# A streaming log-sum-exp: twenty loads in place of nineteen, and the rows' sums dealt out again

## The chip, the core and the metric

The kernel runs on one core of one Trainium2 chip. The metric is device time in microseconds (us), the median of several runs. Five engines matter here: SP (SyncE) issues the transfers, ACT (ScalarE) computes the exponentials, DVE (VectorE) and POOL (GpSimd) sum the rows, and PE (TensorE) does three tiny products at the end. Sixteen DMA engines move the data.

## The reference

The input `x` has 32 x 512 = 16,384 rows of 1,024 numbers in float32, 67.1 MB. For every row the log of the sum of the exponentials is wanted:

```
max_x = np.max(x, axis=-1, keepdims=True)
return max_x.squeeze(-1) + np.log(np.sum(np.exp(x - max_x), axis=-1))
```

The kernel leaves the maximum out at first: it sums the plain exponentials, takes the logarithm, and looks at the end whether every sum lies between 1e-15 and 1e15. Only if one does not, a second pass with the maximum is run, which this input does not need.

## The kernel before, in words

**Layout.** Every one of the 128 partitions holds 128 rows, so a "row" below means one row of 1,024 numbers in each partition, 512 KB in all. The rows pass through a ring in SBUF with room for 48 rows (`RING`). The list `LOADS` is the whole plan: each entry is one transfer, with its size in rows (fractions are allowed) and a string that says what is done with the rows that it completes. Sizes of `before` add up to 128 rows in 19 loads, from 15.6 rows at the start to 0.47 at the end.

**The letters.** `R9` means: one exponential over nine rows on ACT (line 229, in place), then one reduction over the nine rows on DVE (line 240, nine sums). `G5` means: the exponential, then POOL adds the two halves of each of the five rows (line 235), and DVE later sums the halves that are left, 512 numbers a row (line 159). `H` is the place in DVE's order at which all such folded rows are summed. `T2` means: for each of two rows one DVE instruction that adds the two halves and accumulates the row's sum (line 167). `a` and `b` are the last row in two pieces: of `a` DVE adds the halves and accumulates, of `b` ACT itself accumulates during the exponential (line 224). `C` is an early range check on DVE over the sums so far (line 176, two reductions), and `L` the logarithm of the first 112 rows on ACT (line 202), which are then stored while the rest is under way. Parts that are joined by `+` share one exponential.

**Head starts.** A load's size and the rows that it completes need not agree. When a load brings more than the rows that its string names, the exponential covers all that has landed, and the remainder waits in the ring for the next load. So the exponential of a later load can be shorter than the rows that it completes.

**Order.** Each engine works through the plan in its written order; semaphores tie them together. ACT waits for a load's landing (line 188), DVE and POOL for ACT's exponential, DVE for POOL's fold. SP issues the loads in order on one queue (line 141, in the helper `load`). Before a load overwrites a place in the ring, SP waits until DVE has summed the rows that lay there (line 138). If the next load does not fit behind the last one, the ring starts again at its beginning. The first load is issued at the very start, ahead of the program's other preparations.

**`HELD`.** For one load (line 245) DVE waits, before its `T` sums, for the landing of the load after it, and executes an empty instruction.

**The end.** After the last sums, ACT takes the logarithms of rows 112 to 126 (line 267) and of the last row (line 269), and copies one value (line 272); SP stores the last 16 rows; DVE looks at the sums that the early check did not see (lines 278 and 282), PE adds it all up (lines 288 to 292), DVE turns it into a truth value (line 296), and ACT and DVE branch on it.

Of the kernel before, what the change touches and what calls it, by code (L numbers as in the profile page):

```python
# [10 lines left out]
RING = 48  # L11
B = 16

HELD = 15

# [2 lines left out]


LOADS = [
# [5 lines left out]
]  # L28


# [23 lines left out]
def kernel(  # L54
# [125 lines left out]
    for i, (size, parts) in enumerate(loads):  # L180
# [8 lines left out]
        for k, part in enumerate(parts):  # L189
# [41 lines left out]
            for how, s in part:  # L231
# [12 lines left out]
                elif how == "T":  # L244
                    if i == HELD:
                        nc.vector.wait_ge(landed[i + 1], 16)
# [161 lines left out]
```

## Time and profile before

| | before |
|---|---|
| median of 3 runs | 161.53 us (161.51 to 161.56) |
| the profiled execution's own time | 161.49 us |
| its span, first to last instruction | 160.2 us |
| DVE busy | 116.2 us (73%) |
| ACT busy | 114.6 us (72%) |
| POOL busy | 33.3 us (21%) |
| HBM read | 67.11 MB |

The span is the time between the first and the last instruction of the program; the profiled execution's own time is 1.3 us longer. All starts below are in us from the span's start. An engine's busy share is an average over the span: ACT and DVE have nothing to do until the first load has landed, at 21.4 us. Where ACT or DVE instructions follow each other directly, the next one starts a little under 0.1 us before the end of the one before, so the step from start to start is a little less than the duration.

### The profile page before, as it was taken

To read this page: it belongs to the slowest core of one execution; us is meant where nothing else is said; L and a number is where in the kernel's file an instruction comes from. 1 tells how busy PE (TensorE), PEld (TensorE's weight loads), DVE (VectorE), ACT (ScalarE), POOL (GpSimd) and SP (SyncE) were. 2 spreads that over 40 slices of the span, in tenths; PEclk is the share of its full clock that TensorE was granted. 3 is DMA by queue.
4 is the path that set the end of the run, shared out by engine and by line. 5 is a ranking of instruction groups with operands and counts; after the bars stand their busy time and mean duration, and the time that the engine had idled before them with its cause. 6 is when DMAs were issued, how large, how long until landed. Compare 5 with 4: busy or idle time off the path is not lost.

```text
span 160.2 us, 183 instructions
## 1 busy us (share of the span) xinstructions
PE 0.3 (0%) x6; PEld 0.2 (0%) x6; DVE 116.2 (73%) x56; ACT 114.6 (72%) x32; POOL 33.3 (21%) x14
## 2 busy tenths in 40 slices
PE   0000000000000000000000000000000000000000
PEld 0000000000000000000000000000000000000000
DVE  0000000029997599999999699929999999999996
ACT  3000069970999419992799349964998999999996
POOL 0000000000000000000000000990580589996000
DMA  8997999799699699996999999997989999999993
GB/s 272 496 512 336 432 515 466 306 515 498 272 513 513 272 479 478 478 463 268 453 468 468 468 430 430 430 430 332 499 364 472 415 446 395 451 395 431 414 408 105
DMA packets 3025, 67.18 MB, mean 419 GB/s; under 512 B 592, under 2 KB 720, under 8 KB 1488
## 3 DMA queue, kind: packets, MB, share of 16 engines
q1 hardware_dynamic: 3024, 67.18, 97.9%
q14 instruction: 1, 0.01, 0.0%
HBM read 67.11 MB, written 0.07 MB: 419 GB/s over the span
## 4 chain that ended last, share of the span: by engine, by line
DMA 53%; ACT 21%; DVE 18%; POOL 5%; issue 0%; PE 0%; SPq 0%
DMA ring<-in_x_dram 53%; ACT ring L229 21%; DVE sumexp L240 15%; POOL ring L235 5%; DVE sumexp L159 2%; ACT ring L224 0%; SPq L141 0%; DVE clamped L278 0%; PE count L288 0%; ACT res L202 0%; DVE fine L296 0%; PE count L290 0%; PE count L292 0%
## 5 line engine op out<-in xcount | busy, mean ns | idle before, releaser
L229 ACT ACTIVATE ring<-ring 128x16000 f32<-128x16000 f32 (+24 forms) x25 | 112.2, 4546 | 42.7 <-DMA ring<-in_x_dram 42.6
L240 DVE TENSOR_REDUCE sumexp<-ring 128x9 f32<-128x9216 f32 (+7 forms) x10 | 89.8, 9000 | 39.1 <-ACT ring L229 39.1
L235 POOL TENSOR_TENSOR ring<-ring 128x2048 f32<-128x2048 f32 (+5 forms) x8 | 33.0, 4128 | 112.3 <-ACT ring L229 112.2
L159 DVE TENSOR_REDUCE sumexp<-ring 128x4 f32<-128x2048 f32 (+5 forms) x8 | 16.5, 2079 | 3.4 <-POOL ring L235 3.4
L167 DVE SCALAR_TENSOR_TENSOR ring<-ring 128x512 f32<-128x512 f32 (+1 forms) x16 | 9.8, 672 | 0.0
L128 ACT ACT_TABLE_LOAD x1 | 1.3, 1283 | 1.4 <-PEq L63 1.4
L167 DVE DVE_READ_ACCUMULATOR ring<-ring 128x1 f32 x16 | 1.3, 82 | 0.0
L224 ACT ACTIVATE ring<-ring 128x480 f32<-128x480 f32 x1 | 0.6, 602 | 0.0
L288 PE MATMUL count<-far,bad 128*1 128x1 f32 x2 | 0.2, 165 | 158.7 <-DVE clamped L278 158.7
L176 DVE TENSOR_REDUCE sumexp<-sumexp 128x1 f32<-128x106 f32 x2 | 0.4, 260 | 0.0
L296 DVE TENSOR_SCALAR fine<-count 1x1 int32<-1x1 f32 x1 | 0.1, 146 | 0.3 <-PE count L292 0.3
L129 POOL MEMSET ones<- 128x1 f32 x1 | 0.1, 98 | 1.0 <-POOLq L63 1.0
L288 PEld LDWEIGHTS count<-far,bad 128*1 128x1 f32 x2 | 0.1, 82 | 158.7 <-DVE clamped L278 158.7
L202 ACT ACTIVATE res<-sumexp 128x112 f32<-128x112 f32 x1 | 0.3, 280 | 0.0
L269 ACT ACTIVATE res<-rest,sumexp 128x1 f32<-128x1 f32 x1 | 0.3, 261 | 0.0
L278 DVE SCALAR_TENSOR_TENSOR clamped<-sumexp 128x23 f32<-128x23 f32 x1 | 0.2, 183 | 0.1
L267 ACT ACTIVATE res<-sumexp 128x15 f32<-128x15 f32 x1 | 0.2, 205 | 0.0
L290 PE MATMUL count<-total,ones 128*1 128x1 f32 x2 | 0.2, 164 | 0.0
L292 PE MATMUL count<-sumexp,ones 128*1 128x1 f32 x2 | 0.2, 164 | 0.0
L282 DVE TENSOR_REDUCE total<-sumexp 128x1 f32<-128x24 f32 x1 | 0.2, 173 | 0.0
L224 ACT ACTIVATION_READ_ACCUMULATOR ring<-ring 128x1 f32 x1 | 0.2, 153 | 0.0
L272 ACT COPY sumexp<-rest 128x1 f32<-128x1 f32 x1 | 0.2, 151 | 0.0
(8 smaller groups left out, 0.8 us busy)
## 6 DMA issues: line engine op xcount, KB each, us to landing
ring<-in_x_dram SPq DMA_DIRECT2D x1, 8048.0 KB, 38.9
ring<-in_x_dram SPq DMA_DIRECT2D x1, 8016.0 KB, 57.5
ring<-in_x_dram SPq DMA_DIRECT2D x1, 8000.0 KB, 21.4
ring<-in_x_dram SPq DMA_DIRECT2D x1, 7472.0 KB, 25.8
ring<-in_x_dram SPq DMA_DIRECT2D x1, 7312.0 KB, 23.0
ring<-in_x_dram SPq DMA_DIRECT2D x1, 6720.0 KB, 21.6
ring<-in_x_dram SPq DMA_DIRECT2D x1, 5200.0 KB, 17.6
ring<-in_x_dram SPq DMA_DIRECT2D x1, 3584.0 KB, 19.1
```

The source lines that it names most:

```text
L128: nc.scalar.preload_act_table_set("natural_log_exp_and_others")
L159: at = dve.did(nc.vector.reduce_sum(out=sumexp[:, c0 : c0 + s], in_=half, axis=AX.X))
L167: return nc.vector.scalar_tensor_tensor(out=lo, in0=lo, scalar=1.0, in1=v[:, h : 2 * h], op0=ALU.mult, op1=ALU.add, accum_out=sumexp[:, co ...
L176: dve.did(nc.vector.tensor_reduce(out=sumexp[:, col : col + 1], in_=sumexp[:, 0:c], op=op, axis=AX.X))
L202: ln_early = act.did(nc.scalar.activation(out=res[:, 0:W], in_=sumexp[:, 0:W], func=AF.Ln))
L224: nc.scalar.activation(out=v, in_=v, func=AF.Exp, accum_out=rest).then_inc(parts_summed, 1)
L229: at = act.did(nc.scalar.activation(out=v, in_=v, func=AF.Exp))
L235: folded.append((c, p, s, pool.did(nc.gpsimd.tensor_tensor(out=rows[:, :, 0:H], in0=rows[:, :, 0:H], in1=rows[:, :, H:d], op=ALU.add,))))
L240: users.append((p, p + s * d, dve, dve.did(nc.vector.reduce_sum(out=sumexp[:, c : c + s], in_=rows, axis=AX.X))))
L267: act.did(nc.scalar.activation(out=res[:, W:LAST], in_=sumexp[:, W:LAST], func=AF.Ln))
L269: ln_last = act.did(nc.scalar.activation(out=res[:, LAST:NC], in_=rest, func=AF.Ln, bias=sumexp[:, LAST:NC]))
L288: pe.did(nc.tensor.matmul(count, lhsT=bad, rhs=far, start=True, stop=False))
```

## The change

Only the list of loads changes, and with it `HELD`, which names the load that is now number 16 (of 0 to 19). Everything that the list does not say is the same code.

```diff
-HELD = 15
+HELD = 16
 LOADS = [
-    (15.625, "R15"), (15.71875, "R16"), (15.65625, "R9 R7"), (14.59375, "R14"),
-    (14.28125, "G7 H R7"), (13.125, "G5 H R9"), (10.15625, "G4 H R3+G3 H"), (7, "G4 R2 H G1"),
-    (5.84375, "H C G2+R1 G3 H"), (4.46875, "T4"), (3.09375, "T3 L"), (2.40625, "T2"),
-    (1.75, "T2"), (1.25, "T1"), (0.75, "T1"), (0.65625, "T1"), (0.625, "T1"), (0.53125, "a"),
-    (0.46875, "b"),
+    (15.90625, "R15"), (14.71875, "R15"), (15.375, "R16"), (14, "R9 G5 H"), (15.65625, "R8 R7"),
+    (12.34375, "G2+R7 H R4"), (8.9375, "G3 R5"), (6.46875, "G3 G4 H"), (4.09375, "G4"),
+    (4.5, "G2 R2 H T1"), (4.3125, "T4"), (3.0625, "R1+T2 C L"), (2.375, "T2"), (1.78125, "T2"),
+    (1.28125, "T1"), (0.96875, "T1"), (0.6875, "T1"), (0.59375, "T1"), (0.5, "a"), (0.4375, "b"),
 ]
```

The rows are dealt out as follows:

| | before | after |
|---|---|---|
| loads | 19 | 20 |
| `R`, reduced whole on DVE | 83 rows in 10 instructions | 89 rows in 11 |
| `G`, folded on POOL first | 29 rows in 8 | 23 rows in 7 |
| `T`, halves added on DVE | 15 rows in 15 | 15 rows in 15 |
| last row, `a` and `b` | 0.53 and 0.47 of a row | 0.56 and 0.44 of a row |
| exponentials on ACT, `b` included | 26 | 27 |
| early check `C` | over 106 rows, in load 8 | over 119 rows, in load 11 |

The ring starts again after the third load (46 rows; before after the third, 47 rows) and after the sixth (42 rows; before after the sixth). The new list is one line shorter, so all code below it stands one line higher in the changed kernel: its line 228 is line 229 here.

## The prediction

> **What bounds the kernel now.** I read the page first, for the span and the share of the DMA queue, then stretches of the span, then the chain that ended last, then single instructions.
>
> ```profile
> span 160.2 us, 183 instructions
> PE 0.3 (0%) x6; PEld 0.2 (0%) x6; DVE 116.2 (73%) x56; ACT 114.6 (72%) x32; POOL 33.3 (21%) x14
> q1 hardware_dynamic: 3024, 67.18, 97.9%
> ```
>
> The packets of the load queue fill 97.9% of what sixteen DMA engines can do in the span. No compute engine is above 73%. In stretches, where the two numbers at the end of a row are the DMA share and GB/s:
>
> ```profile
> 40.00:80.00 40.00, 0.00 (x0) 0.00 (x0) 37.13 (x3) 30.25 (x4) 0.00 (x0) 1.00 0.97 419
> 80.00:120.00 40.00, 0.00 (x0) 0.00 (x0) 35.36 (x6) 32.03 (x5) 13.42 (x2) 1.00 0.99 430
> 120.00:157.00 37.00, 0.00 (x0) 0.00 (x0) 36.95 (x40) 35.73 (x17) 19.53 (x6) 1.00 1.00 425
> ```
>
> A packet is counted where it starts, so single stretches wobble, but from 40 to 157 us the share is 0.97 to 1.00: the queue never runs dry. In the last stretch DVE is busy for 36.95 of 37 us and ACT for 35.73. Three things are tight there, not one. The chain of waits says the same:
>
> ```profile
> 119.65 23.72 DMA ring<-in_x_dram
> 143.39 6.75 ACT ring L229 x2
> 150.15 0.19 ACT res L202
> 150.33 7.45 ACT ring L229 x7
> 157.78 0.61 ACT ring L224 x2
> ```
>
> By the chain the end is ACT's, but the last load shows how closely the transfers run beside it:
>
> ```profile
> 139.15 3.66 SPq L141 DMA_DIRECT2D ring<-in_x_dram  x1
> ```
> ```profile
> ring<-in_x_dram SPq DMA_DIRECT2D x1, 240.0 KB, 18.5
> ring<-in_x_dram SPq DMA_DIRECT2D x1, 5200.0 KB, 17.6
> out_dram<-res SPq DMA_DIRECT2D x1, 8.0 KB, 1.4
> ```
> ```profile
> 21.45 13.54 ACT L229 ACTIVATE ring<-ring 128x16000 f32<-128x16000 f32 x1 [18.72 <-DMA ring<-in_x_dram]
> 59.34 13.65 ACT L229 ACTIVATE ring<-ring 128x8864 f32<-128x8864 f32 x2 [5.33 <-DMA ring<-in_x_dram]
> 157.72 0.60 ACT L224 ACTIVATE ring<-ring 128x480 f32<-128x480 f32 x1
> 158.41 0.26 ACT L269 ACTIVATE res<-rest,sumexp 128x1 f32<-128x1 f32 x1
> 157.89 0.43 DVE L167 SCALAR_TENSOR_TENSOR ring<-ring 128x272 f32<-128x272 f32 x1
> ```
>
> The last load (240 KB) lands 18.5 us after 139.15, so at 157.65 to 157.70, and ACT starts on it at 157.72. ACT cannot start sooner than the landing whatever is done for its backlog. DVE's last sum ends at 157.89 + 0.43 = 158.32; ACT's read of `b` ends at 157.78 + 0.61 = 158.39, and line 269 starts at 158.41. So the landing sets the end, with ACT and DVE less than 0.1 us from doing so.
>
> **The price of one more load.** Landings 0 and 2 stand 59.34 - 21.45 = 37.89 us apart, for 31.375 rows in two loads. Landing 9 (119.65 + 23.72 = 143.37) and landing 18 (157.65 to 157.70) stand 14.28 to 14.33 us apart, for 11.53 rows in nine loads. With r us a row and f a load: 31.375 r + 2 f = 37.89 and 11.53 r + 9 f = 14.28 to 14.33 give r = 1.205 and f = 0.043 to 0.049. So a load costs 0.05 us of the queue beyond its bytes. The bytes stay the same, so the last landing moves from 157.70 to 157.75. The Trainium skill, "DMA: Bandwidth & Descriptors", section "Anatomy of one DMA", gives about 2.0 us for each DMA plus bytes at 436 GB/s (for the path through GpSimd); r is 524,288 bytes in 1.205 us, 435 GB/s, so the rate agrees, while the fixed part, paid in full for the added load, would make the sum 163.5 us. That it is 0.05 here shows that it lies under the neighbouring transfers.
>
> **ACT after the change.** Counted back from 157.75 with r and f, loads 9 to 19 land at 138.01, 143.25, 146.98, 149.89, 152.08, 153.68, 154.89, 155.76, 156.53, 157.18 and 157.75.
>
> ```profile
> 150.24 2.24 ACT L229 ACTIVATE ring<-ring 128x2464 f32<-128x2464 f32 x1
> 152.38 2.84 ACT L229 ACTIVATE ring<-ring 128x1792 f32<-128x1792 f32 x2
> 155.86 0.75 ACT L229 ACTIVATE ring<-ring 128x672 f32<-128x672 f32 x1
> 156.52 0.72 ACT L229 ACTIVATE ring<-ring 128x640 f32<-128x640 f32 x1
> L229 ACT ACTIVATE ring<-ring 128x16096 f32<-128x16096 f32 x1 | 13.6, 13617 | 5.4 <-DMA ring<-in_x_dram 5.4
> ```
>
> From start to start, 2464 columns take 2.14 us and 672 take 0.66: 0.83 ns a column and 0.095 us. Started 0.02 after a landing, or after the step before, the exponentials of loads 10 to 19 (4416, 3136, the logarithm with 0.19, 2432, 1824, 1312, 992, 704, 608, 512, 448 columns) begin at 143.27, 147.05, 149.95 (after the logarithm), 152.10, 153.72, 154.91, 155.83, 156.55, 157.20 and 157.77. ACT is never more than 0.07 us behind a landing, and for the last load it waits for the landing. `b` shrinks by 32 columns, 0.03 us: the exponential ends at 157.77 + 0.58 = 158.35, against 157.72 + 0.60 = 158.32 now.
>
> **DVE after the change.** It gets six rows more to reduce whole and six fewer to sum after a fold.
>
> ```profile
> L240 DVE TENSOR_REDUCE sumexp<-ring 128x16 f32<-128x16384 f32 x1 | 17.2, 17219 | 2.9 <-ACT ring L229 2.9
> L240 DVE TENSOR_REDUCE sumexp<-ring 128x9 f32<-128x9216 f32 x2 | 19.5, 9744 | 0.0
> L240 DVE TENSOR_REDUCE sumexp<-ring 128x7 f32<-128x7168 f32 x2 | 15.2, 7610 | 0.0
> L159 DVE TENSOR_REDUCE sumexp<-ring 128x2 f32<-128x1024 f32 x1 | 1.2, 1209 | 0.0
> L167 DVE SCALAR_TENSOR_TENSOR ring<-ring 128x512 f32<-128x512 f32 x15 | 9.4, 688 | 0.0
> L235 POOL TENSOR_TENSOR ring<-ring 128x2048 f32<-128x2048 f32 x2 | 9.1, 4538 | 6.5 <-ACT ring L229 6.5
> L235 POOL TENSOR_TENSOR ring<-ring 128x1024 f32<-128x1024 f32 x1 | 2.4, 2364 | 0.1
> ```
> ```profile
> 149.72 0.69 DVE L167 SCALAR_TENSOR_TENSOR ring<-ring 128x512 f32<-128x512 f32 x1
> 150.33 0.69 DVE L167 SCALAR_TENSOR_TENSOR ring<-ring 128x512 f32<-128x512 f32 x1
> 122.33 9.74 DVE L240 TENSOR_REDUCE sumexp<-ring 128x9 f32<-128x9216 f32 x1
> 126.10 4.55 POOL L235 TENSOR_TENSOR ring<-ring 128x2048 f32<-128x2048 f32 x1 [6.54 <-ACT ring L229]
> 144.19 0.43 DVE L176 TENSOR_REDUCE sumexp<-sumexp 128x1 f32<-128x106 f32 x2
> 144.54 1.21 DVE L240 TENSOR_REDUCE sumexp<-ring 128x1 f32<-128x1024 f32 x1
> ```
>
> A reduction takes 1.042 ns a column and 0.15 us, 0.08 less as a step: 1.067 us a row against 0.533 for a folded one, so 6 x 0.533 = 3.2 us more in all, from 116.2 to 119.4 us. A `T` step is 0.61. Up to load 3 DVE waits for ACT, whose exponentials take 0.833 ns a column and 0.2 us: load 0 is 0.28 rows larger and lands 0.34 later, at 21.8, + 13.8 for 16288 columns, + 16.15, so R15 ends at 51.8; load 1 at 39.5 + 12.8 + 16.15, R15 to 68.5; load 2 at 58.1 + 13.3 + 17.2, R16 to 88.7. Then R9 ends at 98.4 and G5 at 101.1, and from there it is busy without a break: R8 109.7, R7 117.2, R7 124.7, G2 125.9, R4 130.2, R5 135.6, G3 137.3, G3 138.9, G4 141.1. R2 waits for load 9's exponential (load 9 lands at 138.0, 1536 and 2048 columns) until 141.3, and ends at 143.5; G4 145.7, G2 146.8, five `T` 149.9, R1 151.0, two `T` 152.3, the check 152.6 (0.38, and 0.03 for 13 more columns), two `T` 153.9, two 155.1, one 155.7. Then DVE waits 0.2 us for load 15's exponential (155.83 - 0.92 + 1.03 = 155.94) and follows ACT: 155.96, 156.63, 157.27, and `a` (288 columns, 0.02 longer) at 157.88 to 158.34. That is 158.32 now, and 0.06 before ACT's read of `b` at 158.41. `HELD` asks for load 17's landing at 156.53, and its sum starts at 156.63 anyway: no cost. The smaller final check (10 columns for 23) takes 0.01 off lines 278 and 282, beside ACT's copy.
>
> **POOL.** Six folds fewer; 4.54 us for four rows, 2.36 for two. The last ones start at 129.5 (G3), 133.4 (G4), 137.9 (G4) and 142.4 (G2), and end at 132.9, 137.9, 142.4 and 144.8; DVE comes to them at 137.3, 138.9, 143.5 and 145.7. The smallest margin is 0.9 us.
>
> **SP and the ring.** One issue more, of 0.33 to 0.45 us on SP, long before it is needed. For the waits on the ring I compare the issue with the landing of the load before it.
>
> ```profile
> 104.82 0.33 SPq L141 DMA_DIRECT2D ring<-in_x_dram  x1
> 110.13 11.50 ACT L229 ACTIVATE ring<-ring 128x4224 f32<-128x4224 f32 x2 [3.37 <-DMA ring<-in_x_dram]
> ```
>
> Now the smallest lead is load 6's: 110.1 - 104.8 = 5.3 us, and the queue stayed full. After: load 3 waits for R15 (51.8) while load 2 lands at 58.1, lead 6.3; load 4 for 68.5 against 75.0, 6.5; load 5 for 88.7 against 93.9, 5.2; the later ones 10 or more. No wait starves the queue, and I cost them at nothing.
> The first load has 65,152 bytes a partition, more than any transfer seen (64,384). If its pieces were cut in two, that is at most one more load's fixed part, 0.05; nothing else in the rows prices it, and I take 0.
>
> **The sum**, against the profiled execution's 161.49 us: + 0.05 for the load, - 0.03 for the shorter `b`, 0 for the rest: 161.51. The median of the runs is 161.53, 0.04 above, so I forecast **161.55 us**. A measurement of this kernel can tell about 0.2% (0.3 us) from no change; this lies well inside.
>
> **Rivals.** (1) *VectorE becomes the bound* (slower). The early check now sits before the last nine `T` sums, and DVE has only the 0.2 us at load 15 and the 0.06 at the end to lose. It decides once DVE, from 101 us on, is more than 0.3 us later than replayed. With 57 us of reductions there, 1.5% would do: 0.85 late gives 161.55 + 0.55 = 162.1. Against it: of the two R9, mean 9744 ns, the one at 122.33 had POOL's fold of 126.10 beside it and took 9.74 us, no more than the other. (2) *The ring starves the queue* (slower): SP comes late to load 5. The last row of issues gives the price of a transfer with nothing beside it, 1.4 us for 8 KB: 162.95. It decides if DVE's R16 is over 4 us late, which 17.2 us of a known row exclude nearly. (3) *ACT is the bound, and even loads free it* (faster): the chain names seven exponentials without a gap. But ACT's `b` starts at most 0.07 after the landing, so with the shorter `b` the gain is at most 0.1: 161.45. For more than 0.3 the transfers themselves would have to run faster. (4) *A load's fixed part lies on the path*: DMA by DMA the 1.4 us above, 162.9; the share of 1.00 to 157 us speaks against it. The section of the Trainium skill named above, "DMA: Bandwidth & Descriptors", has this rule with 2.0 us.
>
> **How the numbers follow.** The forecast, with (3)'s small gain inside it, has 0.81: 161.4 to 161.7. (1) has 0.11, (2) 0.03, (4) 0.01; 0.04 is left for transfers that run faster by over 0.3. So faster 0.04, within 0.2% 0.81, slower 0.15. The range reaches from the gain of (3) to half of (1): 161.35 to 161.85.
>
> **What would show it.** Right: a queue share of 1.00 up to 157 us, the last landing near 157.75, ACT's last exponential 0.02 after it, DVE's gap of 0.2 us before load 15's sum, the check at 152.3. Wrong: DVE's `T` sums back to back to the end and line 269 waiting for line 167; or a dip of the DMA share near 58, 75 or 94 us.

## The result, and the profile after

| | before | after |
|---|---|---|
| median (11 runs each) | 161.53 us | 162.00 us (161.83 to 162.15) |
| ratio | | 1.0029, 95% interval 1.0021 to 1.0038 |
| profiled execution, its span | 161.49, 160.15 | 162.00, 160.43 |
| own time minus span | 1.34 | 1.57 |

The change makes the kernel 0.47 us slower; the forecast was 161.55 and no change. The last row of the table already holds half of it: between the two profiled executions the span grew by 0.28 us, and another 0.23 us lies outside the first and the last instruction of the program.

The page of the changed kernel, then its stretches (the last two numbers are the DMA share and GB/s):

```profile
span 160.4 us, 185 instructions
PE 0.3 (0%) x6; PEld 0.2 (0%) x6; DVE 119.3 (74%) x56; ACT 114.9 (72%) x33; POOL 26.6 (17%) x13
q1 hardware_dynamic: 3168, 67.18, 97.7%
```
```profile
40.00:80.00 40.00, 0.00 (x0) 0.00 (x0) 36.42 (x3) 30.52 (x3) 0.00 (x0) 1.00 1.01 437
80.00:120.00 40.00, 0.00 (x0) 0.00 (x0) 40.00 (x6) 32.07 (x7) 7.95 (x2) 1.00 0.98 422
120.00:157.00 37.00, 0.00 (x0) 0.00 (x0) 36.57 (x40) 34.88 (x17) 18.26 (x5) 1.00 1.00 423
```

DVE's busy time rose by 3.1 us, POOL's fell by 6.7, and the queue is as full as before. Nothing starves. The end of the chain of waits, the issue of the last load with its landing, and the end of ACT and DVE:

```profile
143.43 6.60 ACT ring L228 x2
150.03 0.19 ACT res L201
150.22 7.86 ACT ring L228 x7
158.08 0.56 ACT ring L223 x2
```
```profile
138.49 3.78 SPq L140 DMA_DIRECT2D ring<-in_x_dram  x1
```
```profile
ring<-in_x_dram SPq DMA_DIRECT2D x1, 224.0 KB, 19.5
```
```profile
157.99 0.58 ACT L223 ACTIVATE ring<-ring 128x448 f32<-128x448 f32 x1
158.66 0.26 ACT L268 ACTIVATE res<-rest,sumexp 128x1 f32<-128x1 f32 x1
152.54 0.46 DVE L175 TENSOR_REDUCE sumexp<-sumexp 128x1 f32<-128x119 f32 x2
155.36 0.68 DVE L166 SCALAR_TENSOR_TENSOR ring<-ring 128x512 f32<-128x512 f32 x1
156.21 0.69 DVE L166 SCALAR_TENSOR_TENSOR ring<-ring 128x512 f32<-128x512 f32 x1 [0.15 <-ACT ring L228]
```

The last load lands at 138.49 + 19.5 = 157.97 to 158.0, and ACT starts on it at 157.99. The compute engines keep up, as replayed: DVE even waits 0.15 us for load 15. Inside the span it is the landing that is late: 157.97 where 157.75 was forecast and before had 157.70.

### The profile page after: what moved, and what is told of

It reads as the page before. It is cut to its first block, busy times and chain, and to the rows that moved or that the text cites. A ratio compares the mean times of both kernels' runs of the same rounds, so it can differ in the third digit from the quotient of the medians.

```text
span 160.4 us, 185 instructions
## 1 busy us (share of the span) xinstructions
PE 0.3 (0%) x6; PEld 0.2 (0%) x6; DVE 119.3 (74%) x56; ACT 114.9 (72%) x33; POOL 26.6 (17%) x13
## 4 chain that ended last, share of the span: by engine, by line
DMA 40%; DVE 29%; ACT 26%; another core or an unknown queue 4%; PE 0%; SPq 0%; issue 0%
DMA ring<-in_x_dram 40%; DVE sumexp L239 27%; ACT ring L228 25%; DVE sumexp L158 2%; ACT ring L223 0%; SPq L140 0%; DVE clamped L277 0%; PE count L287 0%; ACT res L201 0%; DVE fine L295 0%; PE count L289 0%; PE count L291 0%
## 5 line engine op out<-in xcount | busy, mean ns | idle before, releaser
L228 ACT ACTIVATE ring<-ring 128x16288 f32<-128x16288 f32 (+25 forms) x26 | 112.6, 4382 | 42.6 <-DMA ring<-in_x_dram 42.6
L239 DVE TENSOR_REDUCE sumexp<-ring 128x15 f32<-128x15360 f32 (+8 forms) x11 | 96.2, 8779 | 39.5 <-ACT ring L228 39.5
L234 POOL TENSOR_TENSOR ring<-ring 128x1024 f32<-128x1024 f32 (+3 forms) x7 | 26.2, 3755 | 117.1 <-ACT ring L228 117.1
L158 DVE TENSOR_REDUCE sumexp<-ring 128x2 f32<-128x1024 f32 (+3 forms) x7 | 13.0, 1896 | 0.0
L223 ACT ACTIVATE ring<-ring 128x448 f32<-128x448 f32 x1 | 0.6, 576 | 0.0
L175 DVE TENSOR_REDUCE sumexp<-sumexp 128x1 f32<-128x119 f32 x2 | 0.5, 272 | 0.0
```

The lines of the kernel that those rows point to most:

```text
L158: at = dve.did(nc.vector.reduce_sum(out=sumexp[:, c0 : c0 + s], in_=half, axis=AX.X))
L175: dve.did(nc.vector.tensor_reduce(out=sumexp[:, col : col + 1], in_=sumexp[:, 0:c], op=op, axis=AX.X))
L223: nc.scalar.activation(out=v, in_=v, func=AF.Exp, accum_out=rest).then_inc(parts_summed, 1)
L228: at = act.did(nc.scalar.activation(out=v, in_=v, func=AF.Exp))
L234: folded.append((c, p, s, pool.did(nc.gpsimd.tensor_tensor(out=rows[:, :, 0:H], in0=rows[:, :, 0:H], in1=rows[:, :, H:d], op=ALU.add,))))
L239: users.append((p, p + s * d, dve, dve.did(nc.vector.reduce_sum(out=sumexp[:, c : c + s], in_=rows, axis=AX.X))))
```

## The experiments

Each was timed against the kernel before on the same chip, whose median there lay between 161.50 and 161.60 us. Medians are of 11 runs, or 12 (e7), 7 (e11) and 5 (e3). "Outside" is the mean of own time minus span over all runs of a kernel. The short edits below leave out what stays the same; three points mark a list that goes on.

**First round: which part of the plan.** Row 112 is a load's end in both plans, so their heads and tails can be exchanged.

```diff
 e1: nothing changed        e2: the changed kernel
 e3: first 9 loads of before (without its C), last 10 of after
 e4: first 10 loads of after, last 10 of before ("C T4" in place of "T4")
```

> The kernel before, once more, timed against itself. If the 0.47 us of the change are real, this gives a ratio of 1.000 with an interval that excludes 1.002; if two builds of one plan can differ by that much, it lies off 1.000 by 0.001 to 0.003. In its profile it also shows by how much the first landing (21.43 in the profile of before) and the last (157.70) move between executions of one plan.

> The changed kernel, on the same chip as the other three. Theory head (the loss is made in the first 112 rows) and theory tail (in the last 16) both expect 162.0 us, ratio 1.003. If the loss belonged to the chip that it was measured on, 161.55.

> The first nine loads of before (112 rows, without the early check) and the last ten loads of after (16 rows, with its check). Theory head: as before, 161.55. Theory tail (VectorE's late check and the smaller steps at the end cost it): as after, 162.0. Should both halves carry a part, in between, near 161.8.

> The first ten loads of after (112 rows) and the last ten of before (16 rows, the early check ahead of the first T sums, over 112 rows). Theory head: as after, 162.0, with the first landing near 21.85 and the landing of the 112th row 0.2 us later than in before. Theory tail: 161.55.

| | median, us | ratio (95%) | outside |
|---|---|---|---|
| e1 | 161.52 | 0.9995 (0.9986 to 1.0004) | 1.34 |
| e2 | 161.97 | 1.0020 (1.0011 to 1.0030) | 1.58 |
| e3 | 162.65 | 1.0062 (1.0048 to 1.0075) | 1.53 |
| e4 | 161.85 | 1.0017 (1.0008 to 1.0026) | 1.57 |

e2 repeats the loss (161.97 against 161.60 of before in this round), and e1 shows that two builds of one plan do not differ by as much. The head alone, e4, carries 0.25 us, and nearly all of that lies outside the span. e3 came out worse than either plan, which no theory expected, and for a reason of its own. Its early check, and the end of its chain of waits:

```profile
153.41 0.46 DVE L190 TENSOR_REDUCE sumexp<-sumexp 128x1 f32<-128x119 f32 x2
```
```profile
153.87 2.70 DVE ring L181 x9
156.57 0.27 issue
156.84 2.31 DVE ring L181 x9
159.15 0.02 issue
159.18 0.19 DVE clamped L292 x2
```

Here DVE is the bound, with its `T` sums back to back to the end, while ACT's last exponential started at 157.82. With the old head DVE comes to the check at 153.41, 0.87 us later than in the changed kernel (152.54), and the new tail has nine sums behind the check. So heads and tails cannot be exchanged one by one, and e3 says nothing of the change's own loss. It does show the prediction's first rival at work: the last logarithm starts at 159.18 instead of 158.66 because DVE is 0.87 us later.

**Second round: what comes with the twentieth load.**

```diff
 e5:  -(14.59375, "R14")          +(7.59375, "R7"), (7, "R7")
 e6:  -range(len(loads))          +range(len(loads) + 1)      (the semaphores of the landings)
 e7:  +nc.sync.nop(nofuse=True)   twice, ahead of the second load
 e8:  -(15.625, "R15"), (15.71875, "R16")   +(15.90625, "R15"), (15.4375, "R16")
```

> Before, with its fourth load (14.59 rows, R14) cut into two (7.59 and 7 rows, R7 each): twenty loads, everything else as it is, far from the end and with idle time on ACT and DVE behind it. In the profiles of the changed kernel and of the mixed one with twenty loads the execution's own time is 1.57 us longer than the span, in before and its repeat 1.33 to 1.34: 0.23 us that no instruction of the span shows. Theory load (they come with the twentieth load): 161.53 + 0.05 in the queue + 0.23 outside the span = 161.8, own time minus span 1.57. Theory plan (they come from something else in the new plan): 161.6, own time minus span 1.34.

> Before, with one semaphore more that nothing uses, inside the range that is cleared at the end. Theory semaphore (the part outside the span is paid for each semaphore of the program): own time minus span 1.57, time 161.75. Theory load or plan: as before, 161.53 and 1.34.

> Before, with two empty instructions more on SP ahead of the second load, as many as SP's program grows by in the changed kernel. Theory code (the length of SP's program sets what is paid outside the span): 161.75, own time minus span 1.57. Otherwise 161.53 and 1.34; the empty instructions themselves lie under the first load's 20 us.

> Before, with the first load as large as in the changed kernel (15.90625 rows, 65,152 bytes a partition) and the second smaller by as much (15.4375). In the span, the first landing of the kernels with the large first load stood at 21.80 to 21.97 against 21.40 to 21.48, 0.34 of which is its 0.28 rows. Theory first landing (the large first load loses another 0.1 us that the queue never regains): 161.63, the last landing 0.1 later than in before. Theory rate (the loss in the span is spread over the loads): 161.53.

| | median, us | ratio (95%) | outside |
|---|---|---|---|
| e5 | 161.77 | 1.0016 (1.0007 to 1.0025) | 1.56 |
| e6 | 161.58 | 1.0005 (0.9996 to 1.0013) | 1.35 |
| e7 | 161.55 | 0.9998 (0.9990 to 1.0007) | 1.35 |
| e8 | 161.52 | 0.9999 (0.9991 to 1.0008) | 1.33 |

One load cut in two, far from the end, costs all of the 0.23 us outside the span and next to nothing in it. A spare semaphore does not bring it, and the large first load costs nothing that can be told. e7 decides less than it was meant to: its page lists 183 instructions, as before's does, while one transfer or one exponential more makes 184 (e12, e17 below). So the profile does not show that the empty instructions were executed. That SP's program does not bring the 0.23 us rests on e12, e14 and e16 below, which issue twenty transfers and have 1.34 to 1.35 outside.

**Third round: the borders between the loads, and a load without an exponential.** In the traces each load has sixteen landing marks, one for each DMA engine. I took the mean of the sixteen, its step from load to load, and took off the prediction's 1.205 us a row. What is left is a load's price beyond its bytes. Most prices agree within 20 ns between executions of one plan (that of before's tenth load does not: 36 to 123 ns). They differ from load to load, mostly from 20 to 90 ns, and sort by where a load begins and ends: sizes are multiples of 128 bytes a partition, and a border can lie at an even multiple (256 bytes) or an odd one. e9 to e11 move borders by 128 bytes and nothing else; in e9 and e11 the last border is among them, so `b` is 32 columns longer there.

```diff
 e9 (after):    -(14.71875, (15.375, (14, (15.65625, ...   +(14.6875, (15.40625, (14.03125, (15.625, ...
 e10 (before):  -(15.625, (15.71875, ...                   +(15.59375, (15.75, ...
 e11 (before):  -(15.71875, (15.65625, (14.59375, ...      +(15.6875, (15.6875, (14.5625, ...
 e12 (before):  load 3 issued as two transfers on one semaphore, and
                -act.wait(landed[i], 16)   +act.wait(landed[i], 32 if i == 3 else 16)
```

> The changed kernel with each border between loads that lies at an even multiple of 128 bytes in a partition's rows moved by 128 bytes to an odd one, except where the ring or the output needs a whole row: 3 even borders of 19, where it has 13. Theory border (from the landings so far: a border at a multiple of 256 bytes costs the queue about 0.04 us more than one between; before has 8 even of 18, after 13 of 19, so 0.19 us of the loss): 162.0 - 10 x 0.038 = 161.6. Theory sizes (the loads of the new plan lose time for another reason): 162.0.

> Before, moved in the same way: 3 even borders of 18, where it has 8. Theory border: 161.53 - 5 x 0.038 = 161.34, faster than before. Theory sizes: 161.53.

> Before with all 18 borders at even multiples (its last load then has 0.5 rows, 0.03 us more of ACT's exponential). Theory border: 161.53 + 10 x 0.038 + 0.03 = 161.94. Theory sizes: 161.56.

> Before with its fourth load issued as two transfers (7.59 and 7 rows) on one semaphore, and still one exponential and one sum over the 14 rows: twenty transfers, and the programs of ACT, DVE and POOL as in before. The 0.23 us outside the span came with the twentieth load where it also brought one more exponential, one more sum and one more semaphore. Theory transfer (SP's or the queue's part of it pays): own time minus span 1.57, 161.77. Theory compute (the longer ACT or DVE program pays): 1.34, 161.55.

| | median, us | ratio (95%) | outside | even borders | price of all loads after the first |
|---|---|---|---|---|---|
| before (seven executions) | | | 1.34 | 8 of 18 | 0.84 to 0.99 us |
| after, e2 | 162.00, 161.97 | 1.0029, 1.0020 | 1.57, 1.58 | 13 of 19 | 1.07, 1.07 |
| e9 | 161.84 | 1.0015 (1.0006 to 1.0024) | 1.56 | 3 of 19 | 0.87 |
| e10 | 161.49 | 0.9995 (0.9986 to 1.0004) | 1.34 | 3 of 18 | 0.83 |
| e11 | 162.04 | 1.0029 (1.0017 to 1.0040) | 1.34 | 18 of 18 | 1.31 |
| e12 | 161.54 | 1.0001 (0.9992 to 1.0010) | 1.35 | | |

e11 is the clearest: the same nineteen loads, each border moved by at most 128 bytes, and the kernel is 0.47 us slower (0.41 expected, 0.03 of it for the longer last exponential), because the last landing is later:

```profile
156.97 1.30 ACT L243 ACTIVATE ring<-ring 128x640 f32<-128x640 f32 x2
158.25 0.63 ACT L238 ACTIVATE ring<-ring 128x512 f32<-128x512 f32 x1
```

ACT's last exponential starts at 158.25, against 157.72 in before. In e11 each load behind the first has a price of 59 to 86 ns, but for the last with 43. e9 gained 0.13 where 0.38 was expected (161.84 against e2's 161.97, on another chip), and e10 0.08 where 0.19 was (161.49 against 161.57 of before in this round); e10's interval does not tell it from no change. So the border theory holds in sign, but ten borders were worth more in e11 than in e9. Averaged by class, loads with two odd borders had 36 ns, with one even 52, with both even 69 (92, 183 and 74 loads of all traces but e12's; the end of the last load counts as even). e12 leaves the outside at 1.35 with twenty transfers. What pays outside the span is not the transfer.

**Fourth and fifth round: the twenty-seventh exponential.**

```diff
 e13 (before):                 +nc.scalar.nop(nofuse=True)  at ACT's start
 e14 (after):                  -"G2 R2 H T1"   +"G2+R2 H T1"     (26 exponentials)
 e15 (e10):                    -"G4 R2 H G1"   +"G4 R2+G1 H"     (25)
 e16 (e9):                     -"G2 R2 H T1"   +"G2+R2 H T1"     (26)
 e17 (before): exponential of load 0 in two pieces               (27)
 e18 (before): exponential of load 0 in three pieces             (28)
```

> Before, with one empty instruction more on ACT at its start, ahead of the 21 us that ACT waits for the first landing. Theory ACT program (its length decides over the 0.23 us outside the span: 26 exponentials 1.34, 27 exponentials 1.57): own time minus span 1.57, 161.76. Theory wait (the twentieth landing that ACT waits for, with its semaphore, costs it): 1.34, 161.54.

> The changed kernel with two of its exponentials in one (of load 9, G2 R2 becomes G2+R2; POOL comes to that fold only at 142.6, after the joined exponential would end): twenty loads and landings, 26 exponentials as in before. Theory ACT program: own time minus span 1.34, 161.98 - 0.23 = 161.75. Theory wait: 1.57, 161.98.

> Before with its borders at odd multiples of 128 bytes (161.49), and two exponentials of load 7 in one (R2 H G1 becomes R2+G1 H; the order of all sums stays): 25 exponentials. Theory ACT program, if every instruction pays: own time minus span 1.11, 161.26, faster than before. If it is a step between 26 and 27: 1.34, 161.49.

> Both repairs on the changed kernel: borders at odd multiples of 128 bytes (161.84) and 26 exponentials. Theory border and theory ACT program together: 161.84 - 0.23 = 161.61, the loss against before all but gone. Theory wait: 161.84.

> Before with the exponential over its first load cut into two halves of 8000 columns: 27 exponentials, and the transfers, landings, borders and sums of before; the 0.1 us that the cut costs ACT lie ahead of idle time. Theory ACT program (the 27th instruction that computes pays 0.23 us outside the span, though an empty one did not): own time minus span 1.57, 161.78. Theory wait (only one that waits for a landing pays): 1.34, 161.55.

> The same with the first exponential in three: 28 exponentials. If what is paid outside the span is a step between 26 and 27, own time minus span is 1.57 as with 27, 161.78; if each one pays, 1.8, 162.0; by theory wait 1.34, 161.55.

| | exponentials | median, us | ratio (95%) | outside |
|---|---|---|---|---|
| e15 | 25 | 161.52 | 1.0000 (0.9991 to 1.0009) | 1.34 |
| e13 (26 and an empty one) | 26 | 161.57 | 1.0002 (0.9993 to 1.0011) | 1.33 |
| e14 | 26 | 161.77 | 1.0014 (1.0005 to 1.0024) | 1.34 |
| e16 | 26 | 161.59 | 1.0001 (0.9992 to 1.0010) | 1.34 |
| e17 | 27 | 161.76 | 1.0016 (1.0007 to 1.0025) | 1.57 |
| e18 | 28 | 161.82 | 1.0019 (1.0010 to 1.0028) | 1.70 |

This settles what brings the 0.23 us, though not why. In e17 transfers, landings and sums are those of before, and one more exponential, 21 us after the start and with 5 us of idle time behind it, makes the kernel 0.26 us slower, all of it outside the span. Its span is not longer:

```profile
span 160.1 us, 184 instructions
```
```profile
21.47 13.63 ACT L233 ACTIVATE ring<-ring 128x8000 f32<-128x8000 f32 x2 [18.74 <-DMA ring<-in_x_dram]
40.43 13.62 ACT L235 ACTIVATE ring<-ring 128x16096 f32<-128x16096 f32 x1 [5.33 <-DMA ring<-in_x_dram]
```

25 and 26 exponentials have 1.34 outside, 27 have 1.57 and 28 have 1.70, so it is neither one step nor a price from the first on: it begins after the 26th. e13 decides nothing: its page has 183 instructions, as before's has, so the empty one may not have been executed. An exponential also adds one to the count on which the other engines wait for ACT; no run separates the two. With both repairs, e16, the changed plan with its twenty loads is as fast as before:

```profile
157.73 0.60 ACT L239 ACTIVATE ring<-ring 128x480 f32<-128x480 f32 x1
158.43 0.26 ACT L284 ACTIVATE res<-rest,sumexp 128x1 f32<-128x1 f32 x1
```

Its last exponential starts at 157.73, 0.26 us earlier than in the changed kernel and 0.01 later than in before. No variant was faster than before by more than the intervals can tell.

## Why the prediction was wrong, point by point

- **"0 for the rest" around the span: the step that failed, 0.23 us.** The sum was made against the profiled execution's own time, 161.49 us, as if the 1.34 us between it and the span could not move. They moved to 1.57 with the 27th exponential. The change's table names that exponential; I priced its 0.095 us on ACT, found it covered by the landings, and looked no further. No row of before could price it, so it ought to have been an unknown with a bound of its own. e14 takes the exponential out of the changed kernel and has 1.34 again; e17 puts it into before and has 1.57. What happens there is not in the trace. The Trainium skill, "Runtime: NRT & Kernel Launch", section "Instruction fetch mechanics", says that an engine's program is fetched in blocks and that a taken branch out of the fetched window has to wait for a fetch. An end that depends on the length of ACT's program would fit that, but no run here shows that a fetch is the cause: the one packet of the instruction queue (`q14 instruction: 1`) starts at 157.92 in before and at 157.93 in e17.
- **"A load costs 0.05 us of the queue beyond its bytes", so the last landing moves to 157.75: mis-sized.** It came at 157.97 and 158.07 (e2), and the price of all loads after the first is 1.07 us against 0.84 to 0.99, 0.1 to 0.2 more. My 0.05 was right as a mean of the loads of before, but loads differ, mostly from 20 to 90 ns, and the new plan has 13 of its 19 borders at multiples of 256 bytes instead of 8 of 18. Moving borders alone gave back 0.13 us (e9 against e2) and 0.18 (e16 against e14, on one chip). A twentieth load as such costs next to nothing in the span (e5; e16 beside before). The Trainium skill, "DMA: Bandwidth & Descriptors", section "How a descriptor splits into AXI transactions", has it that a descriptor that does not start at a multiple of 256 bytes costs more beats. Here the loads with borders at such multiples are the dear ones, 69 ns against 36, and the measurement decides.
- **ACT: right.** The last exponential was to start 0.02 us after its landing, and starts at 157.99, at the end of the row's 157.97 to 158.0. It is 0.03 shorter (0.58 for 0.60).
- **DVE: right, to 0.2 us over 57 us of replay.** R2 was forecast at 141.3 and came at 141.48; the check at 152.3 and came at 152.54, moved by the landings; then a wait for load 15, 0.2 forecast and 0.15 measured. `a` was to end 0.06 before ACT's read of `b`, and ended at 158.60 against 158.63.
- **POOL and the ring: right.** The issue that had the least lead forecast, load 5's, came at 88.82 for a landing of the load before at 94.06, 5.2 us ahead as worked out. The rows are these:

```profile
88.82 0.33 SPq L140 DMA_DIRECT2D ring<-in_x_dram  x1
94.08 7.03 ACT L228 ACTIVATE ring<-ring 128x8192 f32<-128x8192 f32 x1 [6.67 <-DMA ring<-in_x_dram]
141.48 2.29 DVE L239 TENSOR_REDUCE sumexp<-ring 128x2 f32<-128x2048 f32 x1 [0.24 <-ACT ring L228]
```

- **The rivals.** (1), DVE as the bound, did not happen here, though e3 shows that it would with DVE 0.87 us later; there the last logarithm came 0.52 us later than in the changed kernel, and (1) had reckoned 0.55 for 0.85. (2) did not happen. (3), the gain from a freed ACT, did not either: in both kernels ACT's last exponential starts 0.02 us after its landing. (4) named the right place, the fixed part of a load, with the wrong size and for the wrong reason: e12's twentieth transfer costs nothing that can be told (ratio 1.0001).
- **The range.** It ended at 161.85 because it was built from the rivals that the rows could price. Two small costs of one sign, 0.23 and some 0.2 us, were in none of them.

## What to carry to other kernels

Where three resources are balanced to 0.1 us, replaying the engines answers only for the engines: check how the measured time stands to the span, and treat both the mean price per transfer and the time outside the span as unknowns that a new plan can move. An instruction that is hidden in the span may still be paid after it. Before crediting or blaming a plan, change its incidental properties alone (the number of instructions, the borders' places): here these explained the loss that the plan's own idea did not.

## What the runs showed of the hardware

- **More than 26 exponentials on ACT are paid outside the span of this program.** 25 and 26 exponentials: 1.34 us; 27: 1.56 to 1.58 (five kernels); 28: 1.70. A spare semaphore (e6) and one more transfer (e12) leave it at 1.35. Two things stay open. One is the mechanism: whether it is the length of ACT's program or the count that each exponential adds to. The other is why e3, with 26 exponentials, has 1.53: there DVE's last instruction ended later than SP's, and its page is the only one of the twenty without the row of the instruction queue.
- **A transfer's price beyond its bytes depends on its borders.** On average 36 ns with two borders at odd multiples of 128 bytes, 52 with one at a multiple of 256, 69 with both, over transfers of 0.44 to 16 rows. Why, and why the gain from odd borders in before (e10) was smaller than this, was not settled.
